# Seven products for more chunk pairs, and for the down projection, in a decoder layer's two feed-forwards

## The chip, the cores and the metric

One NeuronCore of a Trainium2 chip runs one program. The metric is device time in microseconds (us): of three runs of the kernel before, the median is 2303.18 us, the lowest 2300.65 and the highest 2307.29. Engines are named as in the profile: PE is TensorE (matmuls; PEld its weight loads), DVE VectorE, ACT ScalarE, POOL GpSimd, SP the engine whose queue issues most of the transfers.

## The reference

A hybrid decoder layer on 256 tokens of width 2048, float32: a feed-forward, a mixer (sliding-window attention beside an RWKV-7 recurrence, gated and merged), a cross-attention into 256 memory tokens, a second feed-forward and a final norm. The change touches the feed-forwards alone:

```python
def rms_norm(x, g):
    y = x * lax.rsqrt(jnp.mean(x * x, axis=-1, keepdims=True) + NORM_EPS)
    return y * g
def swiglu(h, w_gate, w_up, w_down):
    return (jax.nn.silu(h @ w_gate) * (h @ w_up)) @ w_down
x = x + 0.5 * swiglu(rms_norm(x, ffn1_norm), ffn1_w_gate, ffn1_w_up, ffn1_w_down)
...
x = x + 0.5 * swiglu(rms_norm(x, ffn2_norm), ffn2_w_gate, ffn2_w_up, ffn2_w_down)
return rms_norm(x, final_norm)
```

Gate and up are 2048 x 5632, down is 5632 x 2048.

## The kernel before

**Splitting.** TensorE multiplies operands of type `float32r`. To keep float32's precision every operand is split into a high part (`hi`, a cast on ScalarE, L324) and a low part (`lo`, the rest, a subtraction on VectorE, L325), and a product of a 128x128 block of activations (stationary) with a 128x512 block of weights is three matmuls: high with high, high with low, low with high (`times`, L394 to L399). Activations are split once; weights are loaded raw and split as they stream through.

**Order of the work.** `weight_plan` (L94) lists all products of the program in order, and items of two 128-row chunks (`KU` = 2, a chunk pair) are cut from it. `next_item` (L358) hands out the next item: it issues loads of coming items on SP's queue (`load`, L301), splits the item itself (`divide`, L346) and the next one (`AHEAD` = 2: two units of two chunks, that is one gate-and-up item). Buffers set how far this runs ahead: three each of `hi` and `lo` (pool `w`), four raw tiles of 1 MB (`raw2`) in the feed-forwards. A second list of work, generators in `Interleave` (L53), is stepped at each `bg.tick()`: transposes of finished blocks, norms, combinations of x. When the program is traced, instructions get their order on each engine from their place in this order and from the time at which they are expected to be ready; that order is then fixed.

**A feed-forward** (`feed_forward`, L590) works in three groups of the 11 column blocks of 512 (4, 4 and 3). Block 0 is done as two plain products. Each of the other ten is one pass over gate and up at once (`product_pair`, L449): 8 chunk pairs q, in each of them 8 products (2 chunks x 2 token halves x gate and up), 24 matmuls. For the pairs in `SEVEN` = (0, 2) it does 7 products instead, by the scheme of Strassen and Winograd over the 2x2 blocks (chunk x token half) and (chunk x gate/up). That takes four sums of the raw weights (`sums`, L328: four subtractions of 128x512 on VectorE, then casts to `thi` and subtractions to `tlo`, one buffer each) and four sums of x (`combinations`, L409, made once per feed-forward). Seven banks p1 to p7 collect the products: p1, p3, p5 in PSUM tag `mm` (3 buffers), p2 and p4 in `acc` (3), p6 and p7 in `tr` (2, shared with the transposes). After the last pair in `SEVEN` three additions (L500 to L502) form what the other banks lack; the remaining pairs add into p2 to p5 (gate and up of both token halves), with a difference of x in p3 for pairs between (`EARLY`). After pair 7 six VectorE operations and two Silus finish the block (L516 to L526), into `hb`. Two VectorE buffers `u` hold what is in between; `combinations` uses the same ones. The block is then transposed into `h` (`hhi`, `hlo`, L542 and L543).

After each group, **down** runs as four plain products of 512 columns (`product`, L375): for each chunk pair of `h` 4 products, 12 matmuls, and at the end of a block two VectorE operations add half of it to x (L635). In the last group of the second feed-forward `done2` and `gain` (L1362) follow; `gain` loads the final norm's weights with POOL's queue into two `raw` buffers, which `sums` uses too.

Of the kernel before, what the change touches and what calls it, by code (L numbers as in the profile page):

```python
# [15 lines left out]
P = 128  # L16
# [18 lines left out]
AHEAD, LOADED = 2, 4  # L35


SEVEN = (0, 2)
EARLY = tuple(q for q in range(max(SEVEN)) if q not in SEVEN)

# [41 lines left out]
def feed_forward_plan(wg, wu, wd):  # L82
    for j0, nj in GROUPS:
        for j in range(j0, j0 + nj):
            if j == 0:
                for w in (wg, wu):
                    yield w, 0, KD, j * 512, 512
            else:
                yield (wg, wu), 0, KD, j * 512, 512
        for n in range(4):  # L90
            yield wd, 4 * j0, 4 * nj, n * 512, 512
# [37 lines left out]
def decoder_layer(ctx: ExitStack, tc: tile.TileContext, a: dict, out: bass.AP):  # L129
# [152 lines left out]
    plan, units, items, ends = [], [], [], []  # L282
    for entry in weight_plan(a):
        if entry is None:
            ends.append(len(units))
            continue
        plan.append(entry)
        w, k0, nk, c0, n = entry
        if not isinstance(w, tuple):
            for k in range(k0, k0 + nk, KU):  # L290
                items.append((len(units),))
                units.append((w, k, c0, n))
            continue
        for k in range(k0, k0 + nk, 2 * KU):
            u = len(units)
            units += [(v, k + i, c0, n) for v in w for i in (0, KU)]
            items += [(u, u + 2), (u + 1, u + 3)]
# [3 lines left out]
    def load(u, pieces=None):  # L301

        if u >= len(units) or u in raws:
            return
        w, k, c0, n = units[u]
        wide = at["pool"] is not None and (u < ends[0] or u >= ends[1] + LOADED)
        m = 2 if wide else 1
        if wide:
            raw = at["pool"].tile([P, m * KU, n], F32, tag="raw2", name="raw2", bufs=4)
        else:  # L310
            raw = wp.tile([P, KU, n], F32, tag="raw", name="raw", bufs=4)
        for i in range(m):
            raws[u + i] = raw[:, i * KU : (i + 1) * KU, :]
        for i, queue in pieces or ((slice(0, m * KU), nc.sync),):
            rows = slice((k + i.start) * P, (k + i.stop) * P)
            queue.dma_start(raw[:, i], w[rows, c0 : c0 + n].rearrange("(a p) n -> p a n", p=P))

    def split_unit(u, rows=slice(0, KU)):
        n, raw = units[u][3], raws[u]
        hi = wp.tile([P, KU, n], F32R, tag="hi", name="hi")  # L320
        lo = wp.tile([P, KU, n], F32R, tag="lo", name="lo")
        for s in (slice(0, 1), slice(1, 2)) if u < AHEAD else (rows,):
            with tc.issue_after(first.ins) if u < AHEAD else nullcontext():
                act.copy(hi[:, s], raw[:, s])  # L324
            dve.tensor_tensor(lo[:, s], raw[:, s], f32(hi[:, s]), ALU.subtract)  # L325
        return hi, lo

    def sums(g, u):  # L328


        sp, rg, ru = at["pool"], raws[g], raws[u]
# [3 lines left out]
        dve.tensor_tensor(ta[:, 0], ru[:, 0], rg[:, 0], ALU.subtract)  # L335
        dve.tensor_tensor(ta[:, 1], ru[:, 1], ru[:, 0], ALU.subtract)
        dve.tensor_tensor(tb[:, 0], ru[:, 1], ta[:, 0], ALU.subtract)
        dve.tensor_tensor(tb[:, 1], rg[:, 1], tb[:, 0], ALU.subtract)  # L338
        for i, t in enumerate((ta, tb)):
            act.copy(hi[:, 2 * i : 2 * i + 2], t[:])  # L340
            dve.tensor_tensor(  # L341
                lo[:, 2 * i : 2 * i + 2], t[:], f32(hi[:, 2 * i : 2 * i + 2]), ALU.subtract
            )
        return hi, lo

    def divide(i):  # L346
        if i >= len(items) or i in parts:
            return
        if len(items[i]) == 1:
            parts[i] = split_unit(items[i][0])  # L350
            return
        g, u = items[i]
        if units[g][1] // KU in SEVEN:
            parts[i] = split_unit(g), split_unit(u, slice(1, 2)), sums(g, u)
        else:
            parts[i] = split_unit(g), split_unit(u)

    def next_item():  # L358
        i = at["item"]
        at["item"] += 1  # L360
        u = items[i][0]
        for v in range(u, u + (2 * LOADED if at["pool"] is not None else LOADED)):
            load(v)
        divide(i)
        room = AHEAD
        for j in range(i + 1, min(i + 1 + AHEAD, len(items))):
            room -= len(items[j])
            if room < 0:
                break
            for v in items[j]:  # L370
                load(v)
# [29 lines left out]
    def multiply(o, x, u, k, t, nk):  # L401
        s = slice(t * P, (t + 1) * P)
        for i in range(KU):
            times(
                o, [x.at(p, k + i)[:, s] for p in range(2)], [w[:, i, :] for w in u],
# [3 lines left out]
    def combinations(sp, norm):  # L409


        x, n = norm.x, 4 * len(SEVEN) + 2 * len(EARLY)
        parts = [sp.tile([P, n, P], F32R, tag="c" + e, name="c" + e) for e in ("hi", "lo")]
        c = {"parts": parts, "at": {}, "done": False, "next": []}

        def work():
            o = 0
            while norm.r is None:
                yield
            for q in range(max(SEVEN) + 1):  # L420
# [6 lines left out]
                if q in SEVEN:  # L427
# [8 lines left out]
                yield  # L436
                s = slice(o, o + n)
                act.copy(parts[0][:, s], f[:, :n])
                yield
# [4 lines left out]
            c["done"] = True  # L444
# [4 lines left out]
    def product_pair(sp, x: Act, c, r, w):  # L449
# [6 lines left out]
        assert pw[0].tensor is w.tensor  # L456
        at["product"] += 1
        b, begun = {}, set()
        hb = sp.tile([P, 2, 512], F32, tag="hb", name="hb", bufs=2)
        u2, u3 = (sp.tile([P, 512], F32, tag="u", name="u", bufs=2) for _ in range(2))  # L460
        late = nk // KU - 1
# [972 lines left out]
```

## Time and profile before

| | us |
|---|---|
| median of three runs | 2303.18 |
| profiled execution, span from first to last instruction | 2304.2 |
| PE busy in the span | 2281.5 |
| PEld / DVE / ACT / POOL busy | 1873.4 / 1514.8 / 1146.6 / 131.8 |
| mean granted TensorE clock | 0.995 |
| first feed-forward, about | 8 to 734 |
| mixer and cross-attention, about | 734 to 1576 |
| second feed-forward, about | 1576 to 2296 |

The profile gives the profiled execution's span and no time beside it. In rows of the timeline a time is the start from the span's beginning, then the duration; L397 to L399 are the three matmuls of a product, whichever product it is, so the written tile (`mm`, `acc`, `tr`) tells the bank. Matmul durations (0.39 us) overlap; the pace is read from starts.

### The profile page before, as it was taken

What the parts mean: (1) busy time and instruction counts of PE and PEld (TensorE: products, weight loads), DVE (VectorE), ACT (ScalarE), POOL (GpSimd) and SP (SyncE); (2) the same over time, 40 slices, a digit from 0 to 9 for tenths busy, and PEclk for the clock granted to TensorE, in tenths of its full rate; (3) what the DMA queues carried; (4) which work ended last, traced back from release to release, by engine and by line L of the source; (5) the groups of instructions that cost most, each with busy time, mean ns of one, the idle gap of its engine ahead of it and who ended that gap; (6) DMA issues with size and microseconds to landing.
All of it is one profiled execution on the core that took longest, in us unless ns stands there. A gap on an engine that the chain in (4) does not pass through costs nothing.

```text
span 2304.2 us, 27723 instructions
## 1 busy us (share of the span) xinstructions
PE 2281.5 (99%) x10751; PEld 1873.4 (81%) x10751; DVE 1514.8 (66%) x1806; ACT 1146.6 (50%) x1532; POOL 131.8 (6%) x193
## 2 busy tenths in 40 slices
PE   9999999999999999999999999999999999999998
PEld 7888888888888877788888888887888888888786
DVE  6775678657865477895444466556875677747765
ACT  6554445434545467544344446555554455534544
POOL 2000000000000000201220030001000000000001
PEclk9999999999999999999999999999999999999999
DMA  7555555555564544676423576557555555555553
GB/s 257 184 203 197 183 202 200 188 196 192 210 228 143 164 128 138 196 228 210 142 85 101 165 258 228 190 162 266 181 203 191 184 209 183 202 199 184 201 201 128
DMA packets 219236, 432.73 MB, mean 188 GB/s; under 512 B 14139, under 2 KB 16416, under 8 KB 219104
## 3 DMA queue, kind: packets, MB, share of 16 engines
q1 hardware_dynamic: 210432, 404.78, 52.1%
q0 software_dynamic: 8208, 25.39, 3.4%
q8 instruction: 84, 1.38, 0.2%
q10 hardware_dynamic: 464, 0.79, 0.1%
q14 instruction: 48, 0.39, 0.1%
HBM read 417.56 MB, written 13.11 MB: 187 GB/s over the span
## 4 chain that ended last, share of the span: by engine, by line
PE 89%; issue 4%; DVE 3%; DMA 2%; ACT 1%; POOL 0%; SPq 0%; POOLq 0%; ACTq 0%; DVEq 0%
PE acc L397 20%; PE acc L398 20%; PE acc L399 20%; PE mm L398 6%; PE mm L399 6%; PE mm L397 6%; PE tr L537 2%; DVE lo L325 1%; PE mm L1133 1%; PE tr L398 1%; PE tr L1102 1%; PE tr L399 1%; PE tr L397 1%; DMA raw<-in_ffn_w_up_dram 1%; ACT hi L324 0%
## 5 line engine op out<-in xcount | busy, mean ns | idle before, releaser
L325 DVE TENSOR_TENSOR lo<-raw,hi 128x1024 fp32r<-128x1024 f32 (+1 forms) x770 | 919.3, 1196 | 670.1 <-ACT hi L324 667.8
L324 ACT CAST hi<-raw 128x1024 fp32r<-128x1024 f32 (+1 forms) x770 | 788.3, 1024 | 945.5 <-PE acc L399 679.7
L397 PE MATMUL acc<-hi,xhi 128*128 128x512 f32 (+1 forms) x1256 | 502.6, 401 | 3.4 <-ACT xhi L564 1.5
L398 PE MATMUL acc<-lo,xhi 128*128 128x512 f32 (+1 forms) x1256 | 491.8, 392 | 4.8 <-DVE lo L325 4.8
L399 PE MATMUL acc<-hi,xlo 128*128 128x512 f32 (+1 forms) x1256 | 490.3, 391 | 0.0
L397 PEld LDWEIGHTS acc<-hi,xhi 128*128 128x128 f32 x1256 | 237.7, 189 | 56.2 <-issue 5.4
L398 PEld LDWEIGHTS acc<-lo,xhi 128*128 128x128 f32 x1256 | 238.4, 190 | 54.9 <-DVE lo L325 6.5
L399 PEld LDWEIGHTS acc<-hi,xlo 128*128 128x128 f32 x1256 | 237.7, 189 | 49.6 <-issue 1.0
L397 PE MATMUL acc<-hi,hhi 128*128 128x512 f32 x704 | 275.0, 391 | 0.0
L399 PE MATMUL acc<-hi,hlo 128*128 128x512 f32 x704 | 274.6, 390 | 0.0
L398 PE MATMUL acc<-lo,hhi 128*128 128x512 f32 x704 | 274.5, 390 | 0.0
L397 PE MATMUL mm<-hi,xhi 128*128 128x512 f32 x480 | 188.0, 392 | 0.0
L399 PE MATMUL mm<-hi,xlo 128*128 128x512 f32 x480 | 187.0, 390 | 0.0
L398 PE MATMUL mm<-lo,xhi 128*128 128x512 f32 x480 | 187.0, 390 | 0.0
L399 PEld LDWEIGHTS acc<-hi,hlo 128*128 128x128 f32 x704 | 132.2, 188 | 27.2
L397 PEld LDWEIGHTS acc<-hi,hhi 128*128 128x128 f32 x704 | 132.2, 188 | 27.0
L398 PEld LDWEIGHTS acc<-lo,hhi 128*128 128x128 f32 x704 | 132.2, 188 | 26.7
L399 PEld LDWEIGHTS mm<-hi,xlo 128*128 128x128 f32 x480 | 90.1, 188 | 18.8
L397 PEld LDWEIGHTS mm<-hi,xhi 128*128 128x128 f32 x480 | 90.2, 188 | 18.4
L398 PEld LDWEIGHTS mm<-lo,xhi 128*128 128x128 f32 x480 | 90.1, 188 | 18.4
L341 DVE TENSOR_TENSOR tlo<-raw,thi 128x1024 fp32r<-128x1024 f32 x80 | 97.0, 1220 | 0.0
L340 ACT CAST thi<-raw 128x1024 fp32r<-128x1024 f32 x80 | 83.5, 1049 | 25.0 <-DVE raw L338 18.3
(347 smaller groups left out, 2527.4 us busy)
## 6 DMA issues: line engine op xcount, KB each, us to landing
raw<-in_ffn_w_up_dram SPq DMA_DIRECT2D x88, 1024.0 KB, 6.6
raw<-in_ffn_w_down_dram SPq DMA_DIRECT2D x88, 1024.0 KB, 5.1
raw<-in_ffn_w_gate_dram SPq DMA_DIRECT2D x84, 1024.0 KB, 5.1
raw<-in_w_in_dram SPq DMA_DIRECT2D x136, 512.0 KB, 3.5
raw<-in_w_out_dram SPq DMA_DIRECT2D x32, 512.0 KB, 4.4
raw<-in_w_proj_attn_dram SPq DMA_DIRECT2D x16, 512.0 KB, 3.5
raw<-in_w_proj_rwkv_dram SPq DMA_DIRECT2D x16, 512.0 KB, 5.9
raw<-in_w_cross_kv_dram SPq DMA_DIRECT2D x16, 512.0 KB, 3.7
```

The source lines that it names most:

```text
L324: act.copy(hi[:, s], raw[:, s])
L325: dve.tensor_tensor(lo[:, s], raw[:, s], f32(hi[:, s]), ALU.subtract)
L340: act.copy(hi[:, 2 * i : 2 * i + 2], t[:])
L341: dve.tensor_tensor(lo[:, 2 * i : 2 * i + 2], t[:], f32(hi[:, 2 * i : 2 * i + 2]), ALU.subtract)
L397: pe.matmul(o, xh, hi, start=first, stop=False, **how)
L398: pe.matmul(o, xh, lo, start=False, stop=False, **how)
L399: pe.matmul(o, xl, hi, start=False, stop=last, **how)
L537: pe.transpose(b[:, o : o + P], tok[:, t, col : col + P], ident[:])
L1102: pe.matmul(b[e][:, m * P : (m + 1) * P], x1[r, j, cs_], x2[r, j, cs_], start=True, stop=True,)
L1133: pe.matmul(vb[:, o : o + P][:, r], lhs(e), rhs[:, r], start=first and e == 0, stop=True, **ek,)
```

## The change

- `SEVEN` becomes (0, 2, 4): three of eight chunk pairs of gate and up take seven products. `EARLY` becomes (1, 3).
- Down takes seven products in pairs 2 and 4 (`SEVEN_DOWN`) of a pair of column blocks: blocks 0 and 1, and 2 and 3, side by side as gate and up were; in the last group only blocks 0 and 1. Sums of `h` are made once a group by the same `combinations`, banks are p1 to p7 and p8 in `acc`. The function `down` adds half of each bank to x, in four operations after pair 4, two 1024-wide additions, and four operations at the end.
- A paired item's raw weights share one tile, rows ordered (g0, u0, u1, g1), filled by two transfers of 512 KB instead of tiles of 1 MB of one matrix. Splits take (g0, u0) and (u1, g1) together; for seven products the order is sums, (u1, g1), g0. Two of the four sums are one 1024-wide subtraction.
- Raw tiles of 1 MB: three instead of four (`RAW`).
- For an ordinary pair the order within it is chunk by chunk over the four banks, no longer bank by bank; `bg.tick()` follows two products as before.
- `combinations` waits some ticks before it starts and between its steps, and a seven-product pair waits for its own combination only, not for all.
- The space for descriptors of software-issued transfers (POOL) is set to 8192.

The diff, cut to its core:

```diff
 AHEAD, LOADED = 2, 4
-
-
-SEVEN = (0, 2)
+RAW = 3
+
+
+SEVEN = (0, 2, 4)
 EARLY = tuple(q for q in range(max(SEVEN)) if q not in SEVEN)
+
+SEVEN_DOWN = (2, 4)
+
+
+def down_pairs(group):
+    return (0,) if group == len(GROUPS) - 1 else (0, 2)
...
+                yield (wg, wu), 0, KD, (j * 512, j * 512), SEVEN
+        for n in (0, 2):
+            if n in down_pairs(gi):
+                yield (wd, wd), 4 * j0, 4 * nj, (n * 512, n * 512 + 512), SEVEN_DOWN
+            else:
+                for m in (n, n + 1):
+                    yield wd, 4 * j0, 4 * nj, m * 512, 512
...
+        if paired(i):
+            raw = raws[i] = at["pool"].tile(
+                [P, 2 * KU, 512], F32, tag="raw2", name="raw2", bufs=RAW
+            )
+            rows = slice(k * P, (k + KU) * P)
+            for v, c, to in zip(w, c0, (raw[:, 0:4:3], raw[:, 1:3])):
+                nc.sync.dma_start(
+                    to, v[rows, c : c + 512].rearrange("(a p) n -> p a n", p=P)
+                )
+            return
...
+        dve.tensor_tensor(ta[:], raw[:, 1:3], raw[:, 0:2], ALU.subtract)
+        dve.tensor_tensor(tb[:, 0], raw[:, 2], ta[:, 0], ALU.subtract)
+        dve.tensor_tensor(tb[:, 1], raw[:, 3], tb[:, 0], ALU.subtract)
...
+        elif items[i][4]:
+            t = sums(raw)
+            u1, g1 = split_raw(raw[:, 2:4], WHOLE)
+            g0, _ = split_raw(raw[:, 0:2], ONE)
+            parts[i] = (g0, g1, u1), t
         else:
+            g0, u0 = split_raw(raw[:, 0:2], WHOLE)
+            u1, g1 = split_raw(raw[:, 2:4], WHOLE)
+            parts[i] = (g0, u0), (g1, u1)
...
+            yield from idle(apart)
+            for q in sorted(seven + early):
+                while not all(KU * q + i in x.done for i in range(KU)):
+                    yield
...
+                yield from idle(2)
                 s = slice(o, o + n)
                 act.copy(parts[0][:, s], f[:, :n])
...
+            u = next_item()
+            for i in range(KU):
+                for to, t, j in (("p2", 0, 0), ("p4", 1, 0), ("p3", 0, 1), (p5, 1, 1)):
+                    off = to == "p3" and q in early
+                    ends = last and i == KU - 1
+                    add(to, of_c(q, i) if off else of_x(t, k + i), u[i][j], ends)
+                    if ends:
+                        finish(to, b)
+                    if t:
+                        bg.tick()
...
+    def down(sp, h, c, w, xs):
+
+
+        hb = sp.tile([P, 2, 512], F32, tag="hb", name="hb", bufs=2)
+        u = sp.tile([P, 2, 512], F32, tag="hb", name="hb", bufs=2)
+
+        def half(o, of, in1):
+            dve.scalar_tensor_tensor(o, of, 0.5, in1, ALU.mult, ALU.add)
+
+        def after(b):
+            act.activation(hb[:, 0], b["p1"][:], AF.Copy, scale=0.5)
+
+        def end(b):
+            half(hb[:, 1], b["p6"][:], hb[:, 0])
+            half(u[:, 0], b["p7"][:], hb[:, 1])
+            half(hb[:, 1], b["p5"][:], hb[:, 1])
+            half(u[:, 1], b["p5"][:], u[:, 0])
+            bg.spawn("ew", residual())
+
+        def residual():
+            for t, v in enumerate((hb, u)):
+                yield
+                o = xs(t, 0, 2)
+                dve.tensor_tensor(o, v[:].rearrange("p a n -> p (a n)"), o, ALU.add)
+
+        def finish(to, b):
+            t, n = {"p2": (0, 0), "p4": (1, 0), "p3": (0, 1), "p8": (1, 1)}[to]
+            half(xs(t, n, 1), b[to][:], xs(t, n, 1))
+
+        product_pair(h, c, w, BANKS | {"p8": acc}, SEVEN_DOWN, (), after, end, finish)
...
+            d = combinations(sp, h, SEVEN_DOWN, (), lambda: True, "d", 0)
+            for n in (0, 2):
+                if n in down_pairs(gi):
+                    down(
+                        sp, h, d, wd,
+                        lambda t, m, w: x[:, t, (n + m) * 512 : (n + m + w) * 512],
+                    )
+                    if end:
+                        done(n)
+                        done(n + 1)
+                    continue
...
+    nc = _bacc.Bacc(
+        "TRN2", target_bir_lowering=False, num_devices=1, dynamic_dma_scratch_size=8192
+    )
```

245 lines of the change are left out of this document (112 added, 133 removed).

## Prediction, made before the result

> **What bounds the kernel now.** I read the page first (span, busy shares, chain), then stretches of the span as a table (the columns PE, PEld, DVE, ACT, POOL give busy us, then granted clock, DMA share, GB/s).
>
> ```profile
> span 2304.2 us, 27723 instructions
> PE 2281.5 (99%) x10751; PEld 1873.4 (81%) x10751; DVE 1514.8 (66%) x1806; ACT 1146.6 (50%) x1532; POOL 131.8 (6%) x193
> ...
> PE 89%; issue 4%; DVE 3%; DMA 2%; ACT 1%; POOL 0%; SPq 0%; POOLq 0%; ACTq 0%; DVEq 0%
> ```
>
> ```profile
> 60.00:734.00 674.00, 674.00 (x3029) 556.96 (x3027) 466.78 (x509) 325.03 (x362) 2.77 (x4) 1.00 0.57 194
> 734.00:1576.00 842.00, 835.24 (x4293) 680.66 (x4292) 509.85 (x686) 437.37 (x722) 100.70 (x131) 1.00 0.55 175
> ...
> 1640.00:2288.00 648.00, 645.94 (x2880) 533.69 (x2879) 444.92 (x475) 307.17 (x335) 11.06 (x10) 1.00 0.55 190
> ```
>
> ```profile
> 187.00:274.00 87.00, 87.00 (x390) 71.79 (x389) 50.38 (x51) 36.23 (x36) 0.00 (x0) 1.00 0.58 193
> ...
> 317.30:360.40 43.10, 43.10 (x196) 35.69 (x195) 34.35 (x40) 22.48 (x25) 0.00 (x0) 1.00 0.57 195
> 306.10:327.70 21.60, 21.60 (x97) 17.87 (x96) 21.45 (x27) 12.61 (x14) 0.00 (x0) 1.00 0.55 191
> ```
>
> TensorE is the bound, and both feed-forwards, the only stages the change enters, run almost without a gap. So every matmul taken away is worth its full pace, until another engine is late. Which one, the last rows say: over one gate-and-up block (43.1 us) VectorE is busy 34.35 us, 80%, but from chunk pair 7 of one block to pair 2 of the next it is busy 21.45 of 21.6 us. There its reserve is used up already.
>
> The pace of a matmul, from the first matmuls of pairs 0, 1 and 2 of a block:
>
> ```profile
> 317.28 0.39 PE L397 MATMUL mm<-hi,xhi 128*128 128x512 f32 x1
> ...
> 322.04 0.39 PE L397 MATMUL acc<-hi,xhi 128*128 128x512 f32 x1
> ...
> 327.48 0.39 PE L397 MATMUL mm<-hi,xhi 128*128 128x512 f32 x1
> ```
>
> Pair 0 (seven products, 21 matmuls) takes 4.76 us, pair 1 (24 matmuls) 5.44 us: 0.2267 us each; the 0.39 us are overlapped durations.
>
> **What goes.** One more pair with seven products saves three matmuls in each of ten blocks per feed-forward: 60 in two. Down gets five paired column blocks per feed-forward (two in groups 0 and 1, one in group 2), two pairs with seven products each: 5 x 2 x 3 x 2 = 60. Together 120 x 0.2267 = **27.2 us**, if nothing is late.
>
> **What VectorE gets for it.** Starts of its operations in a busy run give the pace:
>
> ```profile
> 306.71 0.69 DVE L336 TENSOR_TENSOR raw<-raw 128x512 f32<-128x512 f32 x1
> 307.31 0.69 DVE L337 TENSOR_TENSOR raw<-raw,raw 128x512 f32<-128x512 f32 x1
> 307.92 1.22 DVE L325 TENSOR_TENSOR lo<-raw,hi 128x1024 fp32r<-128x1024 f32 x1
> 309.05 0.69 DVE L338 TENSOR_TENSOR raw<-raw,raw 128x512 f32<-128x512 f32 x1
> 309.65 1.22 DVE L341 TENSOR_TENSOR tlo<-raw,thi 128x1024 fp32r<-128x1024 f32 x1
> ```
>
> A 512-wide operation costs 0.60, a 1024-wide one 1.14. I call the four sums and their low parts S (before 4 x 0.60 + 2 x 1.14 = 4.68; after, with two sums in one 1024-wide operation, 4.62) and the splits beside them D: 1.74 for seven products (1.14 + 0.60), 2.28 for eight. A seven-product pair thus costs VectorE 6.36 us for TensorE's 4.76, an ordinary one 2.28 for 5.44.
>
> How far ahead may VectorE work? Three `hi` buffers:
>
> ```profile
> 301.16 1.05 ACT L324 CAST hi<-raw 128x1024 fp32r<-128x1024 f32 x1 [1.67 <-PE mm L399]
> 303.88 1.05 ACT L324 CAST hi<-raw 128x1024 fp32r<-128x1024 f32 x1 [1.67 <-PE acc L399]
> ```
>
> Each cast waits until TensorE frees a buffer, one per half pair (2.72 us). So a pair's splits come about one pair ahead and no earlier; only S can run ahead, as far as its raw tile has landed.
>
> **Gate and up, time 0 at pair 0.** With three raw tiles pair 2's load leaves when pair 7 is split (-5.7). Landing:
>
> ```profile
> raw<-in_ffn_w_up_dram SPq DMA_DIRECT2D x88, 1024.0 KB, 6.6
> ...
> raw<-in_ffn_w_gate_dram SPq DMA_DIRECT2D x84, 1024.0 KB, 5.1
> raw<-in_w_in_dram SPq DMA_DIRECT2D x136, 512.0 KB, 3.5
> ```
>
> Two issues of 512 KB: between 5.1 (like one of 1 MB) and 2 x 3.5 = 7.0; I take 5.8 with the second issue, so it has landed at 0.1. The finishing of the block before comes later than now, since pair 7 ends with p2, p4, p3, p5 once each (-2.04, -1.36, -0.68, 0). Its six operations:
>
> ```profile
> 314.32 0.68 DVE L516 TENSOR_TENSOR hb<-acc,hb 128x512 f32<-128x512 f32 x1
> 314.92 0.68 DVE L519 TENSOR_TENSOR hb<-acc,u 128x512 f32<-128x512 f32 x1
> ...
> 318.80 0.74 DVE L524 SCALAR_TENSOR_TENSOR hb<-u,rs,hb 128x512 f32<-128x512 f32 x1
> 319.46 2.35 DVE L325 TENSOR_TENSOR lo<-raw,hi 128x1024 fp32r<-128x1024 f32 x2
> ```
>
> Pair 0's last split takes VectorE to -1.5; the six, at 0.60 to 0.66, to 2.2. Then D of pair 1 (to 4.5), S of pair 2 (to 9.1), its D (to 10.9). Pair 2 starts at 4.76 + 5.44 = 10.2 and wants its first low part 0.23 later: the last split is **0.5 us late**. Pair 3's D and pair 4's S and D (2.28 + 6.36 = 8.64) fit into pairs 2 and 3 (10.2). So a block's price lies between 0 and 0.8 us. Would TensorE wait for that last split (g0, for p1)? Its order is fixed at compile time, not always as written:
>
> ```profile
> 61.38 0.39 PE L397 MATMUL mm<-thi,chi 128*128 128x512 f32 x1
> ...
> 62.06 0.44 PE L397 MATMUL tr<-thi,chi 128*128 128x512 f32 x1
> ```
>
> Here p6 (`tr`) runs behind p5 (`mm`), though written three products earlier: its bank was not free. If p7 and p6, whose sums are made first, go ahead of p1, the lateness vanishes. I take 0.2 us: 20 x 0.2 = +4 (ends 0 and 16).
>
> ScalarE gains one wide and one narrow cast a block, under 1.7 us beside 22.48 of 43.1 busy: hidden. The one wait that is added there, the cast into the single `thi` tile, ends when p5 of the last seven-product pair is done; an ordinary pair always lies between, so it ends 5.44 us before TensorE wants the result. Behind it stand the next `hi` casts and the Silus; they would be late by as much as it, and with them VectorE's splits.
>
> **Down.** Rows for what is new there, the first three from a grouping of 1576 to 1640 us:
>
> ```profile
> L423 DVE TENSOR_TENSOR u<-xhi,xlo 128x512 f32<-128x512 f32 x3 | 2.1, 688 | 0.1
> ...
> L440 DVE TENSOR_TENSOR clo<-u,chi 128x512 fp32r<-128x512 f32 x2 | 1.4, 688 | 0.0
> ...
> L429 DVE TENSOR_TENSOR u<-u 128x128 f32<-128x128 f32 x2 | 0.6, 292 | 0.0
> ```
>
> ```profile
> L635 DVE SCALAR_TENSOR_TENSOR x<-acc,x 128x512 f32<-128x512 f32 x48 | 31.2, 684 | 2.1 <-PE acc L399 2.1
> ...
> L543 DVE TENSOR_TENSOR hlo<-tr,hhi 128x512 fp32r<-128x512 f32 x44 | 30.2, 687 | 3.4 <-ACT hhi L542 2.6
> ```
>
> A combination of `h` costs about 2.2 us (0.6 + four of 0.2 to 0.3 + 0.6, pipelined), two a group. In the first pair of a group VectorE has, from 0: five of the six finishing operations 3.1, D of pair 1 2.28, `hlo` 1.3, combinations 4.4, S and D of pair 2 6.36, D of pair 3 2.28, S and D of pair 4 6.36 = 26.1. Pair 4 ends at 25.84 (2 x 5.44 + 4.76 + 5.44 + 4.76); even if p1 went last in it, its low part is wanted 0.45 before, by 25.4. The combinations cannot go earlier: they use the two `u` buffers that the finishing still reads. So at least 0.6 us late, 1.2 to 2 with the order of single products: I take 1.5, 6 first pairs, **+9** (ends 4 and 39; the upper one is the rival below). A second pair has no combinations and finishes with four 0.64 us operations; its last split for pair 2 comes at 10.7 against 11.1: nothing. The hand-over to the next group, +1 in all (0 to 4).
>
> **What may come back.** Two stretches of the second feed-forward lose time now:
>
> ```profile
> 1582.00:1586.00 4.00, 1.37 (x6) 0.51 (x4) 3.86 (x10) 3.44 (x5) 2.14 (x3) 0.96 0.80 278
> 1586.00:1590.00 4.00, 4.00 (x12) 3.14 (x13) 2.65 (x3) 0.38 (x2) 0.00 (x0) 0.61 0.96 339
> ```
>
> ```profile
> 2186.00:2189.50 3.50, 1.44 (x7) 0.86 (x6) 2.64 (x4) 1.05 (x1) 0.00 (x0) 1.00 0.01 4
> 2189.50:2193.00 3.50, 3.50 (x9) 2.77 (x10) 3.50 (x5) 1.04 (x1) 0.00 (x0) 0.55 0.69 222
> ```
>
> ```profile
> 2176.09 1.10 POOL L1367 DMA_DIRECT2D raw<-in_final_norm_dram  x2 [591.95 <-DVE tlo L341]
> ```
>
> ```profile
> 2186.86 0.69 DVE L335 TENSOR_TENSOR raw<-raw,raw 128x512 f32<-128x512 f32 x1 [3.68 <-DMA raw<-in_ffn_w_up_dram]
> ```
>
> The first is VectorE busy with combinations of x while TensorE waits (about 3 us, and 0.39 x 4 = 1.6 by the lower clock behind it). Spread out, that may go: -4.7 to 0, I take -2.3. In the second, POOL's loads of the final gain delay a weight load: about 2.2 + 0.45 x 3.5 = 3.8. The gain's buffers come free elsewhere now: -3.8 to 0, I take -2.
>
> These rows also price a wait: a hole of 2.2 us was followed by 3.5 us at clock 0.55. [...] By the trace, first pairs that wait in one piece would cost 1.6 more each (+9.6, 2295); I expect waits of single products, and leave that case inside the forecast's own range.
>
> Splitting the loads, the strided tile and twice the issues hide behind landings with 2.6 us or more to spare (pair 4's load leaves at 4.5, lands at 10.4 and is wanted at 13); beyond that each us counts in every block. The halved descriptor space touches POOL's transfers alone, and POOL is busy 6% of the span: I take 0, at most one landing, 6.6 us. The two wider `c` combinations (3.9 us more of VectorE) lie in the 43 us of block 0, beside TensorE.
>
> Sum: -27.2 + 4 + 9 + 1 - 2.3 - 2 = -17.5. The page shows no time outside the span; the span stands 1.0 above the median of the three runs, inside their spread. 2304.2 - 17.5 - 1.0 = **2286**; this case's own range is 2277 to 2296.
>
> **Rivals.**
> - All covered: TensorE's order hides every lateness and both lossy stretches heal: -27.2 - 4.7 - 3.8 = -35.7, 2267.5. For: 21.6 us of solid VectorE cost TensorE nothing before. Against: 26.1 us of work due by 25.4 in down's first pairs.
> - Even: each block loses what it saves (20 x 0.68 = 13.6), first pairs 2 each (12), hand-over 1, one lossy stretch half healed (-2): -2.6, about 2301. For: the 0.5 us that the sum above leaves late is nearly that. Against: it holds only without any change of order.
> - Slower: TensorE keeps the written order, so p1 waits for g0, made last. Blocks 0.7 (14), first pairs 3.6 at pair 2 and 1.2 at pair 4 (28.8) plus 1.6 of clock (9.6), hand-over 1: +53.4 - 27.2, 2329. It decides once a first pair loses over 3.9 us. Against: the row of p6.
> - Loads: two 512 KB transfers that do not overlap take 7.0 us against 5.3 per pair, about 1.7 x 236 pairs = 400 us more. Against: gate and up already overlap now. [...]
>
> **Chances.** Forecast 0.47, all covered 0.18, even 0.13, slower in written order 0.17, loads 0.02, other slowdowns 0.03. A difference of 0.3% (6.9 us) is about the least that a measurement can tell: faster 0.65, within 0.13, slower 0.22. The range leaves out the slower case and the loads (0.19) and reaches a little past full cover and even: 2265 to 2316.
>
> **What would show it.** 120 fewer 128x512 matmuls; VectorE near 38 of 42.4 us in a block; TensorE waits on `lo` at pair 2 of blocks and in each group's first down pair; clock 1.00 where holes are short. The forecast is wrong if waits there sum over 27 us, if VectorE waits for `raw` loads, or if VectorE's pace per operation changes.

## The result, and the profile after

| | median us (runs) | lowest to highest |
|---|---|---|
| before, in the same session | 2305.03 (4) | 2300.65 to 2307.29 |
| changed kernel | 2288.12 (4) | 2287.09 to 2291.22 |

The ratio is 0.9929, 95% interval 0.9916 to 0.9941: about 16 us less (the two medians lie 16.9 apart). The profiled execution became 17.0 us shorter, against -17.5 in the prediction's sum. That these agree says little yet: the parts of the sum did not come where the prediction put them.

The page of the changed kernel, the lines that answer to those of before:

```profile
span 2287.2 us, 28425 instructions
PE 2258.0 (99%) x10631; PEld 1847.3 (81%) x10631; DVE 1738.3 (76%) x2116; ACT 1216.8 (53%) x1638; POOL 133.7 (6%) x193
...
PE 86%; DVE 5%; issue 5%; DMA 2%; ACT 2%; SPq 0%; POOL 0%; POOLq 0%; ACTq 0%; DVEq 0%
```

```profile
60.00:734.00 674.00, 671.33 (x2999) 552.00 (x2998) 580.07 (x665) 364.19 (x422) 3.85 (x7) 1.00 0.61 196
734.00:1576.00 842.00, 834.07 (x4283) 678.62 (x4282) 508.76 (x689) 434.76 (x718) 101.30 (x130) 1.00 0.57 174
186.20:271.60 85.40, 85.40 (x380) 70.23 (x379) 78.89 (x94) 44.69 (x49) 0.00 (x0) 1.00 0.62 197
313.30:355.90 42.60, 42.60 (x193) 35.09 (x192) 37.97 (x44) 24.10 (x28) 0.00 (x0) 1.00 0.60 197
653.20:725.10 71.90, 69.78 (x314) 56.73 (x313) 58.27 (x78) 39.75 (x58) 2.25 (x3) 0.98 0.56 188
...
2211.20:2278.50 67.30, 65.15 (x290) 53.34 (x289) 54.57 (x68) 35.02 (x48) 11.80 (x7) 1.00 0.42 141
```

120 matmuls are gone (10751 to 10631). VectorE has 223 us more work, ScalarE 70, and TensorE's share on the chain that ended last falls from 89% to 86%, VectorE's rises from 3% to 5%. In the stretches (columns as in the prediction) a block (313.30) and a down group of four column blocks (186.20) run without a gap; the last groups (653.20 and 2211.20) do not: TensorE is busy 69.78 of 71.90 us and 65.15 of 67.30. VectorE's 37.97 of 42.60 us in a block are the 38 of 42.4 that the prediction named.

So the stages, in us, one profiled execution each. Borders are the starts of the first and the last matmul that reads `h` in each down group; "g0" holds the plain block 0 and three paired ones. The kernels below the second row are those of the experiments.

| kernel | gate and up, first ff: g0, g1, g2 | down, first ff | mixer | gate and up, second ff | down, second ff |
|---|---|---|---|---|---|
| before | 179.08, 171.74, 128.62 | 87.80, 87.80, 68.91 | 838.50 | 178.90, 171.74, 132.59 | 87.78, 87.81, 66.05 |
| changed | 178.19, 169.35, 126.83 | 85.43, 85.40, **71.94** | 840.43 | 177.56, 170.05, 127.20 | 85.43, 85.38, **67.34** |
| changed_again | 177.56, 169.69, 126.99 | 85.42, 85.41, 70.33 | 841.40 | 180.17, 169.61, 127.09 | 85.46, 85.40, 67.33 |
| written_order | 181.78, 169.34, 126.73 | 87.56, 87.56, 70.79 | 838.54 | 181.01, 169.65, 126.76 | 87.58, 87.60, 67.75 |
| last_plain | 177.42, 169.28, 126.72 | 85.42, 85.40, 68.82 | 838.99 | 179.46, 169.51, 126.79 | 85.41, 85.38, 65.96 |
| residual_late | 178.01, 169.25, 126.71 | 85.41, 85.41, 67.72 | 839.82 | 178.39, 169.24, 126.73 | 85.42, 85.38, 65.57 |
| combos_later | 178.22, 169.58, 126.73 | 85.98, 85.93, 70.61 | 837.53 | 173.45, 170.10, 126.72 | 85.95, 85.93, 67.31 |
| gate_up_only | 177.48, 169.56, 128.46 | 87.76, 87.72, 68.87 | 838.33 | 178.33, 169.63, 127.41 | 87.76, 87.73, 66.03 |
| down_only | 179.16, 172.15, 128.82 | 85.38, 85.38, 71.91 | 837.38 | 177.85, 172.03, 128.84 | 85.45, 85.44, 67.35 |
| layout_only | 179.36, 172.03, 128.83 | 87.77, 87.77, 68.82 | 840.97 | 179.74, 171.98, 128.81 | 87.72, 87.77, 65.96 |
| seven_four | 176.01, 169.14, 128.01 | 86.04, 86.05, 72.49 | 839.87 | 179.10, 168.30, 125.87 | 86.35, 86.53, 68.11 |
| best_three | 178.67, 170.13, 126.75 | 85.96, 85.97, 66.31 | 838.42 | 172.71, 169.78, 126.95 | 85.96, 85.97, 66.98 |
| best_two | 177.97, 170.17, 126.74 | 85.45, 85.41, 67.79 | 841.96 | 174.08, 170.02, 127.36 | 85.45, 85.46, 65.63 |
| best_ff1 | 177.84, 169.86, 126.97 | 85.47, 85.41, 66.17 | 839.47 | 174.86, 169.88, 127.15 | 85.41, 85.43, 65.59 |

Without any new wait g1 would fall by 4 x 0.68 = 2.72, g0 and g2 by 2.04, a down group of four column blocks by 2.72, a last group by 1.36. g1 of the first feed-forward fell by 2.39 and groups 0 and 1 of down by about 2.4. The last groups rose, by 3.03 and 1.29.

The rows of the hole in the first of them, TensorE and then VectorE (L575 is a half-addition, L591 a residual addition of `down`, L342 a split):

```profile
685.49 0.39 PE L426 MATMUL acc<-hi,hlo 128*128 128x512 f32 x1
687.99 0.47 PE L424 MATMUL acc<-hi,hhi 128*128 128x512 f32 x1 [2.12 <-DVE x L575]
...
681.23 0.69 DVE L575 SCALAR_TENSOR_TENSOR hb<-tr,hb 128x512 f32<-128x512 f32 x1
...
683.69 1.29 DVE L575 SCALAR_TENSOR_TENSOR hb<-mm,hb 128x512 f32<-128x512 f32 x2
684.89 1.22 DVE L342 TENSOR_TENSOR lo<-raw,hi 128x1024 fp32r<-128x1024 f32 x1
686.03 1.22 DVE L591 TENSOR_TENSOR x<-hb,x 128x1024 f32<-128x1024 f32 x1
687.16 1.28 DVE L575 SCALAR_TENSOR_TENSOR x<-acc,x 128x512 f32<-128x512 f32 x2
688.36 1.21 DVE L591 TENSOR_TENSOR x<-hb,x 128x1024 f32<-128x1024 f32 x1
```

p2, p4 and p8 hold all three `acc` banks, and the plain column block behind needs two. From one matmul's start to the next 2.50 us pass, 2.12 of them idle, until the first finishing half-addition has read its bank, and that stands on VectorE behind other half-additions, a split and a residual addition. In the last group pair 4 is followed by one pair only; groups 0 and 1 have three pairs for the same work. The second feed-forward has the same hole at 2243.46, 2.54 us (2.15 idle). Below, too, the length of a hole is the step from start to start.

### The profile page after: what moved, and what is told of

Its sections match the earlier page's. It is cut to its first block, busy times and chain, and to the rows that moved or that the text cites. A ratio compares the mean times of both kernels' runs of the same rounds, so it can differ in the third digit from the quotient of the medians.

```text
span 2287.2 us, 28425 instructions
## 1 busy us (share of the span) xinstructions
PE 2258.0 (99%) x10631; PEld 1847.3 (81%) x10631; DVE 1738.3 (76%) x2116; ACT 1216.8 (53%) x1638; POOL 133.7 (6%) x193
## 3 DMA queue, kind: packets, MB, share of 16 engines
q8 instruction: 83, 1.36, 0.3%
## 4 chain that ended last, share of the span: by engine, by line
PE 86%; DVE 5%; issue 5%; DMA 2%; ACT 2%; SPq 0%; POOL 0%; POOLq 0%; ACTq 0%; DVEq 0%
PE acc L424 18%; PE acc L425 17%; PE acc L426 17%; PE mm L424 7%; PE mm L425 7%; PE mm L426 7%; DVE lo L342 2%; PE tr L606 2%; PE tr L425 2%; PE tr L426 1%; PE tr L424 1%; DMA raw<-in_ffn_w_up_dram 1%; PE mm L1213 1%; ACT hi L341 1%; PE tr L1182 1%
## 5 line engine op out<-in xcount | busy, mean ns | idle before, releaser
L342 DVE TENSOR_TENSOR lo<-raw,hi 128x1024 fp32r<-128x1024 f32 (+1 forms) x770 | 890.2, 1166 | 394.8 <-ACT hi L341 393.7
L341 ACT CAST hi<-raw 128x1024 fp32r<-128x1024 f32 (+1 forms) x770 | 763.6, 1001 | 791.7 <-PE acc L426 389.6
L360 ACT CAST thi<-raw 128x1024 fp32r<-128x1024 f32 x160 | 165.6, 1051 | 66.9 <-DVE raw L357 33.0
L361 DVE TENSOR_TENSOR tlo<-raw,thi 128x1024 fp32r<-128x1024 f32 x160 | 192.7, 1219 | 1.3 <-ACT thi L360 1.3
L424 PE MATMUL acc<-hi,hhi 128*128 128x512 f32 x452 | 176.9, 394 | 4.3 <-DVE x L575 4.3
L426 PE MATMUL acc<-hi,hlo 128*128 128x512 f32 x452 | 177.3, 392 | 0.0
L425 PE MATMUL acc<-lo,hhi 128*128 128x512 f32 x452 | 177.2, 392 | 0.0
L425 PE MATMUL mm<-lo,xhi 128*128 128x512 f32 x380 | 148.0, 389 | 0.0
L355 DVE TENSOR_TENSOR raw<-raw 128x1024 f32<-128x1024 f32 x80 | 97.7, 1221 | 24.3 <-DMA raw<-in_ffn_w_up_dram 22.7
L424 PEld LDWEIGHTS acc<-hi,hhi 128*128 128x128 f32 x452 | 85.2, 188 | 23.0 <-issue 2.7
L425 PEld LDWEIGHTS acc<-lo,hhi 128*128 128x128 f32 x452 | 85.2, 188 | 19.3 <-DVE lo L342 2.3
L426 PEld LDWEIGHTS acc<-hi,hlo 128*128 128x128 f32 x452 | 85.2, 188 | 17.3
```

The source lines that it names most:

```text
L355: dve.tensor_tensor(ta[:], raw[:, 1:3], raw[:, 0:2], ALU.subtract)
L360: act.copy(hi[:, s], t[:])
L361: dve.tensor_tensor(lo[:, s], t[:], f32(hi[:, s]), ALU.subtract)
L424: pe.matmul(o, xh, hi, start=first, stop=False, **how)
L425: pe.matmul(o, xh, lo, start=False, stop=False, **how)
L426: pe.matmul(o, xl, hi, start=False, stop=last, **how)
```

## The experiments

My theory after the result (A in the expectations): VectorE is late in down's first pairs, as predicted, but the order in which TensorE issues single matmuls hides it; down's loss lies in the last groups' banks. The rival (B): VectorE is not late, and the loss lies elsewhere. All ratios are to the kernel before.

**written_order.** Inside a paired product, each product's three matmuls are put behind those of the product before (`issue_after` puts what it encloses behind an instruction of the same engine):

```diff
-            times(b[to][:], x_, w_, to not in begun, last, skip_group_check=True)
+            with tc.issue_after(chain[-1].ins) if chain else nullcontext():
+                m = times(b[to][:], x_, w_, to not in begun, last, skip_group_check=True)
+            chain.append(m)
```

> The changed kernel, but inside every paired product TensorE is made to take the products in the order in which they are written (each product's three matmuls behind those of the one before). Theory A (VectorE is as late as the prediction worked out, and only TensorE's order, fixed at compile time and mixing single products of several pairs, hides it): TensorE waits for low parts at pair 2 of the blocks (0.7 us each, 14 in all) and at pairs 2 and 4 of each down group's first pair (3.6 and 1.2 us, 29 in all), so 2310 to 2335 us. Theory B (VectorE has slack there and is not late; the order of TensorE does nothing): 2286 to 2291 us, the time of the changed kernel.

Measured: 2299.76 us, ratio 0.9986 (0.9976 to 0.9995), about 12 us of the gain gone. The timeline of a first pair of down, in this kernel and in the changed one (p1's first, second and third matmul are `mm<-hi,hhi`, `mm<-lo,hhi` and `mm<-hi,hlo`; L342 of 512 columns makes the `lo` of g0):

```profile
201.58 0.39 PE L424 MATMUL mm<-hi,hhi 128*128 128x512 f32 x1
203.04 0.50 PE L425 MATMUL mm<-lo,hhi 128*128 128x512 f32 x1 [1.07 <-DVE lo L342]
...
213.30 0.39 PE L424 MATMUL mm<-hi,hhi 128*128 128x512 f32 x1
214.35 0.50 PE L425 MATMUL mm<-lo,hhi 128*128 128x512 f32 x1 [0.67 <-DVE lo L342]
...
202.30 0.69 DVE L342 TENSOR_TENSOR lo<-raw,hi 128x512 fp32r<-128x512 f32 x1
```

```profile
198.00 0.39 PE L424 MATMUL mm<-hi,hhi 128*128 128x512 f32 x1
198.23 0.39 PE L424 MATMUL acc<-hi,hhi 128*128 128x512 f32 x1
198.46 0.39 PE L425 MATMUL acc<-lo,hhi 128*128 128x512 f32 x1
198.68 0.39 PE L426 MATMUL acc<-hi,hlo 128*128 128x512 f32 x1
198.91 0.39 PE L424 MATMUL tr<-thi,dhi 128*128 128x512 f32 x1
...
199.81 0.39 PE L425 MATMUL mm<-lo,hhi 128*128 128x512 f32 x1
...
198.68 0.68 DVE L342 TENSOR_TENSOR lo<-raw,hi 128x512 fp32r<-128x512 f32 x1
```

In written order TensorE waits at pair 2 (a step of 1.46 us in place of 0.23) and at pair 4 (1.05), at the very places where the prediction has VectorE late. In the changed kernel p1 is begun with its high parts at 198.00, seven other matmuls are put between, and the matmul that needs the late `lo` follows at 199.81. Not products are interleaved but their single matmuls. Groups 0 and 1 go from 85.4 back to 87.6: there the order is worth 2.2 us a group. But less came than A expected (2310 and more), for two reasons: the waits are 1.2 and 0.8 us, not 3.6 and 1.2; and the blocks of gate and up lost nothing (g1 169.34 against 169.35), where A had 0.7 each. The rest is 3.6 and 3.5 us in the two g0. Each has one hole of 2.25 us, where p7 waits for a `tr` bank that transposes of block 0 hold, which a free order goes round. Each also has 3.41 us at half clock that the changed kernel did not have there, from 63.89 and from 1586.23; the second fall stands behind holes that the edit did not make. In return two falls of the changed kernel are missing, at 689 (70.79 for 71.94 in that group) and in the mixer: both executions have 10.24 us at half clock before their last 20 us, so the clock alters the 12 us little.

**last_plain.** The last groups' down left plain.

```diff
-    return (0,) if group == len(GROUPS) - 1 else (0, 2)
+    return () if group == len(GROUPS) - 1 else (0, 2)
```

> The changed kernel, with the last group of each feed-forward's down left plain (no paired column blocks there; groups 0 and 1 as changed). Theory A (down's loss of 8 us lies in the last groups, which became 3.03 and 1.29 us longer than before the change): the two last groups go back to 68.9 and 66.1 us, about -4.3, so 2284 us, ratio to before 0.991. Rival (each of the six first pairs lost alike, about 1.4 us of the 2.72 that two of its pairs save): the two last groups' pairs were worth 1.3 each, so 2290 to 2291 us, ratio 0.994.

Measured: 2281.32 us, ratio 0.9903 (0.9888 to 0.9917). The last groups are back at 68.82 and 65.96, groups 0 and 1 stay at 85.4. That is A's theory, though the time fell by more than A's 4.3 us and more than the two groups' 4.5; where the last group has a paired block, that block made the kernel slower.

**residual_late.** The last groups' pair stays, but its two residual additions are issued behind the finishing half-additions.

```diff
-            bg.spawn("ew", residual())
+            if not behind:
+                bg.spawn("ew", residual())
...
-            half(xs(t, n, 1), b[to][:], xs(t, n, 1))
+            i = half(xs(t, n, 1), b[to][:], xs(t, n, 1))
+            if behind and to == "p8":
+                with tc.issue_after(i.ins):
+                    for _ in residual():
+                        pass
```

> The changed kernel, with the last groups' two 1024-wide residual additions put behind the four finishing half-additions of the same paired block. Theory A (the plain block behind waits for two accumulator banks, which VectorE's finishing half-additions free only behind the residual additions): the two holes of 2.5 us shrink by 1.1 to 2.5 us each, and the 1.7 us of low clock behind the first one goes, so 2282 to 2286 us, ratio to before 0.990 to 0.992. Rival (VectorE as a whole is behind there, and the next wait is for the low parts of the plain block's first weights): holes of the same length, now ended by lo, 2287 to 2290 us.

Measured: 2278.96 us, ratio 0.9890 (0.9874 to 0.9907), better than either theory. VectorE's rows at the place of the hole:

```profile
682.56 0.68 DVE L575 SCALAR_TENSOR_TENSOR hb<-tr,hb 128x512 f32<-128x512 f32 x1
683.42 0.69 DVE L575 SCALAR_TENSOR_TENSOR x<-acc,x 128x512 f32<-128x512 f32 x1 [0.18 <-PE acc L426]
684.03 1.28 DVE L575 SCALAR_TENSOR_TENSOR hb<-mm,hb 128x512 f32<-128x512 f32 x2
685.22 1.22 DVE L342 TENSOR_TENSOR lo<-raw,hi 128x1024 fp32r<-128x1024 f32 x1
686.36 0.68 DVE L575 SCALAR_TENSOR_TENSOR x<-acc,x 128x512 f32<-128x512 f32 x1
...
688.15 2.35 DVE L592 TENSOR_TENSOR x<-hb,x 128x1024 f32<-128x1024 f32 x2
```

With the residuals out of the way the first finishing half-addition moved from 687.16 to 683.42, ahead of two others, and the hole is gone altogether. The last groups take 67.72 and 65.57: the pair now earns 1.1 and 0.4 us over plain. The two groups are 4.2 and 1.8 us shorter than in the changed kernel, 1.6 of the first by the clock (see changed_again), and VectorE's total work there is the same: the wait for the bank was the cause. The residual addition itself stood for 1.13 us of the delay (686.03 to 687.16); the rest came because the compile-time order of the other half-additions changed with the edit.

**combos_later.** The sums of x, on VectorE, behind the split issued last, begun later, and with one step between (which, through the shared function, holds for the sums of h too).

```diff
+                with tc.issue_after(at["lo"].ins) if apart else nullcontext():
...
-                yield from idle(2)
+                yield from idle(1)
...
-        c = combinations(sp, norm.x, SEVEN, EARLY, lambda: norm.r is not None, "c", 4)
+        c = combinations(sp, norm.x, SEVEN, EARLY, lambda: norm.r is not None, "c", 12)
```

> The changed kernel, with the sums of x for gate and up put, on VectorE, behind the splits that were issued last, and begun 12 steps into the block instead of 4 (and 1 step apart instead of 2). Theory A (at the start of the second feed-forward the cast of the first raw weights stands on ScalarE behind casts of these sums, which wait for VectorE; 3.9 us of TensorE's time): the holes at 1577 and 1579 go, -2 to -4 us, so 2284 to 2286 us, ratio to before 0.991. Rival (the first raw weights have not landed by then): the holes stay, ended by the load, 2288 us. Second rival (the sums come too late for block 1 of the group): a new wait for clo near 1664, 2288 to 2292 us.

Measured: 2283.26 us, ratio 0.9911 (0.9896 to 0.9925), a little below A's 2284. The start of the second feed-forward in the changed kernel, ScalarE (L468 casts a sum, L341 raw weights) and TensorE, then the same place in this kernel as a table of stretches:

```profile
1577.67 0.40 ACT L468 CAST chi<-u 128x256 fp32r<-128x256 f32 x1 [1.22 <-DVE u L465]
1577.98 1.99 ACT L341 CAST hi<-raw 128x1024 fp32r<-128x1024 f32 x2
...
1579.07 0.73 PE L424 MATMUL acc<-hi,xhi 128*128 128x512 f32 x2 [1.48 <-ACT hi L341]
1581.67 0.50 PE L425 MATMUL acc<-lo,xhi 128*128 128x512 f32 x1 [1.86 <-DVE lo L342]
```

```profile
1574.00:1578.00 4.00, 4.00 (x19) 3.31 (x18) 1.48 (x2) 1.76 (x2) 1.84 (x3) 1.00 0.71 214
1578.00:1582.00 4.00, 4.00 (x19) 3.33 (x18) 2.12 (x2) 1.41 (x2) 0.00 (x0) 1.00 1.01 390
```

In the changed kernel the cast of raw weights stands behind a cast of a sum that waits 1.22 us for VectorE, and begins the moment that is done. With the sums behind the splits TensorE has no gap, and g0 falls from 177.56 to 173.45. So the wait was one of order in ScalarE's queue, not of the loads; which of the edit's parts (order, later start, single step) moved the cast was not tried alone. The single step cost down 0.5 us a group (85.9 for 85.4).

**gate_up_only, down_only, layout_only.** The parts alone: down plain everywhere (`down_pairs` returns `()`); `SEVEN = (0, 2)` with down's pairs; both.

> The changed kernel with down left plain everywhere: three seven-product pairs in gate and up, the shared raw tiles and the spread sums stay. Theory A (of the 17 us, gate and up with the two healed stretches give 13.5, down 5.3, and 1.9 are lost in the mixer): the six down groups go back to 87.8 and 66 to 69 us, +5.3 on the changed kernel, 2292 to 2295 us, ratio to before 0.995 to 0.996. Rival (down's pairs cost VectorE time that the blocks of gate and up behind them pay for): the blocks behind get shorter too, 2288 to 2290 us.

> The changed kernel with only two seven-product pairs (0 and 2) in gate and up, as before; down's pairs, the shared raw tiles and the spread sums stay. Theory A: the third pair is worth 20 x 0.68 = 13.6 less some 4 to 5 us of new waits, so 9 us more than the changed kernel, 2296 to 2298 us, ratio 0.996 to 0.997; the wait for low parts of sums in the first paired block of a group (holes of 0.95 and 1.32 us) goes. Rival (each block loses most of what it saves): 2289 to 2292 us.

> The changed kernel with two seven-product pairs in gate and up and down plain: as many matmuls as before, but the shared raw tile with two loads of 512 KB, three raw buffers, the new order of the products and the spread sums. Theory A (the 3.9 us lost at 2187 us go with the new buffers, 0.7 at the start of the second feed-forward with the spread sums; nothing else): 2299 to 2301 us, ratio 0.998. Rival (the smaller loads or the strided tile cost something in every block): 2304 us and more. Second rival (the new order alone gains part of the 17 us): 2296 us and less.

Measured: 2294.91 us, ratio 0.9951 (0.9938 to 0.9964); 2297.87 us, 0.9962 (0.9950 to 0.9974); 2305.16 us, 0.9995 (0.9986 to 1.0005). The first two are as A expects. The third is not: the layout by itself gains nothing, and the rival's 2304 and more came, for the most part not by the rival's mechanism. Its stages tell why: it does heal the stretch at 2187 (g2 of the second feed-forward 132.59 to 128.81, -3.8) but costs 0.07 us a block (g1 172.0 against 171.74), which is what is left of the rival, does not heal the start of the second feed-forward (179.74), and its mixer is 2.5 longer. The gains of the two parts add up within the intervals: 0.49% + 0.38% are more than the whole's 0.71%, by less than they are uncertain. The third pair of gate and up, alone, shortens the two g1 by 2.80 and 1.98 us with down's pairs (changed against down_only) and by 2.47 and 2.35 without (gate_up_only against layout_only): 2.4 of the possible 2.72 in the mean.

**best_three, best_two, best_ff1.** The edits together: residual_late, combos_later and both column blocks of down paired in the first feed-forward's last group; then the first two only, with the sums of h left at two steps; then that with the third again.

> The changed kernel with three edits: the last groups' residual additions behind the finishing half-additions, the sums of x for gate and up later and behind the splits, and in the first feed-forward's last group both column blocks of down paired. If the three add up: 2279 from the first, about -4 from the second (the holes at the start of the second feed-forward), and -1.4 from six matmuls less in the third, so 2272 to 2275 us, ratio 0.986 to 0.988. Rival (the mixer's first product waits for the last two column blocks of x, which now come together): the third edit costs 1 to 4 us instead, 2276 to 2280 us.

> The changed kernel with two edits: the last groups' residual additions behind the finishing half-additions, and the sums of x for gate and up later and behind the splits; unlike in the two kernels before that had the later sums, down's sums of h keep their two steps. Theory A (with one step for the sums of h, each down group of those kernels took 85.93 to 85.97 us in place of 85.41, and the last group's hole came back; the two edits by themselves add up): groups of 85.4 us, last groups of 67.7 and 65.6 us, no hole at the start of the second feed-forward, 2274 to 2276 us, ratio 0.987. Rival (the edits interfere whatever the steps of h): 2279 us as with all three, ratio 0.988 to 0.989.

> The kernel best_two, and in the first feed-forward's last group both column blocks of down paired. Theory A (66.3 us for that group in place of 67.7, with 0.8 us of waiting at the start of the mixer): 0 to 1.4 us less than best_two, 2273 to 2276 us. Rival (the new order of VectorE's work moves a wait elsewhere): 1 to 3 us more than best_two.

Measured: 2278.86 us, ratio 0.9883 (0.9869 to 0.9897); 2280.17 us, 0.9888 (0.9874 to 0.9903); 2278.86 us, 0.9884 (0.9868 to 0.9901). The expectations of 2272 to 2276 failed. For best_three and best_two the rival's times came; best_ff1 lies 1.3 us below best_two, as its A has it, but above A's 2276. None can be told from residual_late alone. In best_two the start of the second feed-forward keeps its gain (174.08 against residual_late's 178.39), groups of down are back at 85.4; but g1 of both feed-forwards takes 0.8 to 0.9 more and the mixer 2.1 more. Why a later sum makes later blocks of gate and up longer stays open.

**seven_four.** `SEVEN = (0, 2, 4, 6)`.

> The changed kernel with a fourth seven-product pair (6) in each of the 20 paired blocks of gate and up: 60 matmuls less again, 13.6 us, for 4.1 us more of VectorE's time in each block. Theory A (VectorE has about 42.55 - 38 = 4.5 us a block left, all of it outside the stretch from pair 0 to pair 4, so four pairs leave it none: 42.1 of 41.9): VectorE becomes the bound and TensorE waits in every block, 0.5 to 2 us each: 2284 to 2315 us. Rival (what is idle on VectorE can be used up to the last, since both orders are interleaved): most of 13.6 is kept, 2275 to 2280 us.

Measured: 2289.51 us, ratio 0.9926 (0.9911 to 0.9941): 60 matmuls less again, worth 13.6 us, and no time gained on the changed kernel. Stretches of g1, first feed-forward, of the changed kernel and of this one:

```profile
271.60:441.00 169.40, 169.40 (x759) 139.71 (x758) 145.12 (x160) 92.72 (x103) 0.00 (x0) 1.00 0.61 199
```

```profile
270.00:439.20 169.20, 167.81 (x747) 137.09 (x746) 160.35 (x178) 97.63 (x111) 0.00 (x0) 1.00 0.61 199
```

The time is within A's range. VectorE goes from 86% to 95% and TensorE begins to wait, for `tlo` (2.9 us in the whole execution, 1.5 in the changed kernel) and for VectorE's finishing additions (4.2 us in six waits, none there): in this stretch the fourth pair gives 0.2 us, in the second feed-forward's g1 1.8, where the third gave 2.4. All gate-and-up stages together are 4.7 us shorter than in changed_again, whose clock fell at the same place there (13.6 were possible), and the down groups 4.65 us longer than in the changed kernel. Four pairs are past the point where VectorE's work can be hidden; three, for the most part, are not.

**changed_again.** The changed kernel once more.

> The changed kernel itself once more, for a second profiled execution and another interval. What is asked: the mixer, which the change does not enter, took 838.5 us before, 840.4 in the changed kernel, and 837.4 to 842.0 in its variants. Theory A (this is the run of its loads and differs from one execution to the next): the holes at 685 and 2243 us come again with 2.5 us each, the last groups again 71.9 and 67.3, but the mixer differs from 840.4 by over 0.5 us, and whether the clock falls behind each hole of some 2.5 us may change. Rival (it belongs to the compiled program): 840.4 within 0.3 us, and the clock falls behind the same hole only. The time within 2286 to 2291 us either way.

Measured: 2289.21 us, ratio 0.9929 (0.9915 to 0.9942), as A expects. The holes came again (2.55 and 2.55 us), the mixer took 841.40. Stretches of the first execution and of this one:

```profile
689.00:693.00 4.00, 4.00 (x15) 3.09 (x14) 3.39 (x5) 0.47 (x1) 1.52 (x2) 0.57 0.98 365
...
2246.00:2250.00 4.00, 4.00 (x18) 3.31 (x19) 3.91 (x5) 3.02 (x7) 2.71 (x2) 1.00 0.62 241
...
1582.00:1586.00 4.00, 4.00 (x19) 3.32 (x18) 3.96 (x7) 1.46 (x2) 0.00 (x0) 1.00 0.73 221
```

```profile
689.00:693.00 4.00, 4.00 (x24) 3.25 (x22) 3.74 (x6) 2.26 (x4) 1.52 (x2) 1.00 0.95 355
...
1580.00:1584.00 4.00, 3.34 (x8) 2.69 (x9) 3.97 (x6) 0.83 (x2) 0.00 (x0) 0.50 0.69 231
1584.00:1588.00 4.00, 4.00 (x14) 3.14 (x13) 2.41 (x5) 1.04 (x1) 0.00 (x0) 0.64 0.59 217
```

The same program with the same holes: the clock (third column from the right) fell behind 685 in one execution and not in the other, and behind the start of the second feed-forward the other way round. The first fall is 3.41 us at half clock (689.08 to 692.49) and cost 1.6 us (71.94 against 70.33); the second is 6.83 us (1580.03 to 1586.86) and cost 2.6 (180.17 against 177.56).

## Why the prediction was right, and where it was not

In the prediction's terms the profiled executions give -27.2 + 4.1 (blocks of gate and up, with the start of the second feed-forward) + 8.4 (down) - 4.0 (final norm's loads) + 1.9 (mixer) - 0.3 (both ends) = -17.1. That this is so near to -17.5 is partly luck: the misses below cancel.

- **120 matmuls, -27.2**: right in count, and as a bound: the third pair shortens g1 by 2.0 to 2.8 of 2.72. The stretch of 21.6 us that the prediction has running from pair 7 starts with pair 6 (TensorE's first matmul of pair 6 is at 306.40, of pair 7 at 311.84); the sum does not use it.
- **Blocks of gate and up, +4**: right in size, not in mechanism. g1 and g2 lost 2.2 us in 14 blocks against the 2.72 and 2.04 possible (g2 of the second feed-forward counted from 128.62, without the stretch at 2187); g0 of the first 1.15, with a hole of 0.95 at 112.59 that waits for `tlo`; g0 of the second 0.7, with such a hole of 1.32 at 1711.68. At pair 2 there was no wait even in written order (g1 169.34). The step "the last split is 0.5 us late" failed: VectorE's order is fixed at compile time too, and the low part of the sums' second half was put behind the split that p1 needs:

```profile
322.72 0.68 DVE L342 TENSOR_TENSOR lo<-raw,hi 128x512 fp32r<-128x512 f32 x1
...
324.46 1.22 DVE L361 TENSOR_TENSOR tlo<-raw,thi 128x1024 fp32r<-128x1024 f32 x1
```

  The first matmul of pair 2 stood at 323.53, its first low part was wanted at 323.75, and the split was done at 323.40. All of VectorE's work for pair 2 was done only at 325.68, 2.15 us into pair 2, so VectorE was no earlier than I had it; what was wrong is which operation comes last and when that one is wanted (`tlo` by p6, behind p1, p2 and p7, at 325.80: 0.1 us to spare).
- **First down pairs, +9**: too much. Groups 0 and 1 lost 0.3 us each. VectorE was late where I said, shown by written_order, by 1.2 and 0.8 us; the order of single matmuls covered it. I had weighed an interleaving of products, not of matmuls within them.
- **Hand-over, +1 (0 to 4)**: the step that failed most. The last groups lost 71.94 - 67.55 = 4.4 and 67.34 - 64.69 = 2.65 us, 7.0 in all, 1.6 of it by the clock. I looked for lateness of weights behind a paired block, and not at what its banks do to the next one; for a plain column block behind a paired one in the same group, the sum has no term at all. residual_late shows the cause. With the first pairs, +10 was forecast for down, and 8.4 came: the right sum from the wrong place.
- **Start of the second feed-forward, -2.3**: not there. The holes grew from 1.88 + 1.53 to 1.87 + 2.26 us; what was saved (178.90 to 177.56) is less than the third pair's 2.04 us together with the fall of the clock (3.41 us at half speed) that stood there before and happened not to come. In the second execution g0 took 180.17. Yields alone did not move the sums out of the way; the explicit order, later start and single step of combos_later together did.
- **Final norm's loads, -2 (0 to -3.8)**: the lower end came. layout_only gives -3.8 by itself, so it comes with the layout; which part of that (buffers, loads, order) was not tried alone. The same clock times in the changed kernel, where POOL's two loads are issued at 2177.73 and 2181.31 and no step of TensorE in all of g2 is longer than 0.51 us:

```profile
2186.00:2189.50 3.50, 3.50 (x17) 2.92 (x16) 2.62 (x3) 0.92 (x3) 0.00 (x0) 1.00 0.79 294
```

- **Mixer, 0**: +1.9 and +2.9 in two executions. Its program isn't touched, and the other kernels with the same smaller descriptor space take 837.4 to 842.0, so that space alone is not the cause. The mixer ran 6.8 us at half clock before, and 6.8 and 10.2 in the two executions, so the clock explains nothing of the first and at most 1.7 us of the second. In layout_only and changed_again the mixer's holes near 975 to 988 us wait for the cast of a raw tile (1.47 us at 985.85 and 1.17 at 977.51), in layout_only for its load (that cast has waited 7.06 us for it at 984.75); the cause stays open.
- The **loads** rival is out: with two transfers of 512 KB a block runs without a gap at 42.6 us. The two smaller loads cost at most the 0.07 us a block of layout_only here. The **slower** rival's mechanism, written order, was real where it was forced, with over a quarter of its price: 12 us for 43 (2329 - 2286).

## What to carry to other kernels

When work is taken from a saturated TensorE and given to VectorE, look at what each added operation holds while it waits in VectorE's queue: here an accumulator bank that an addition had to free was dearer (two holes of 2.5 us) than a late weight (hidden), because the order of matmuls did not go round it, while it did go round a `tr` bank that was held (2.25 us in written_order, where it could not). Put the additions that free banks ahead of those that only store results: in residual_late that took both holes away. A total of work against a deadline overstated the wait here (1.5 us a first pair in the prediction, 0.3 measured in groups 0 and 1), where the compile-time order interleaves single matmuls; whether it does can be seen by forcing the written order.

## What the runs showed of the hardware

The granted clock after a hole was not settled by the hole's length here. Holes of 2.50 and 2.55 us (2.12 and 2.16 idle) at one place of one program were followed by 0.57 in one execution (689 to 693) and 1.00 in the next. In the kernel before and in the changed kernel's first execution every fall that ends before the program's last 20 us is at clock 0.50 and lasts 3.41 us (before from 8.72, 1585.68 and 2189.84; changed from 689.08, 801.72 and 869.98) or 6.83 (before from 807.44); changed_again has one of 6.83 from 1580.03. By half of that, an estimate, such a fall costs at most 1.7 or 3.4 us, and 1.6 and 2.6 were measured.

The prediction priced a fall at 1.6 us for every hole of that size. Behind the hole at 685 this cost came in one execution of two (71.94 against 70.33 us in that group), a difference within the spread of the changed kernel's runs (2287.09 to 2291.22).
